# Retention in a hybrid decoder block: the queries made by seven products, and the sums of seven products made in PSUM

## The chip, the cores and the metric

One core of a Trainium2 chip runs the whole program in one launch. The metric is the device time of one execution in microseconds, with data already in the chip's memory; lower is better. The core has a matrix engine (TensorE, PE in the profile, whose weight loads stand in a row of their own, PEld), two element-wise engines that can read the matrix engine's result banks (VectorE, DVE; ScalarE, ACT), a third that can't (GpSimd, POOL), and a queue that issues most of the DMAs (SyncE, SP). Matrix products land in PSUM, eight banks of 512 numbers per partition; everything else lives in SBUF, 128 partitions wide.

## The reference

A block of a decoder: 512 tokens and 16 learned meta tokens ahead of them, width 1024. The mixers share one normalised input `hn` and one wide projection. The change is in retention, the first of the two mixers (4 heads, keys and queries 256 wide, values and gates 512 wide):

```python
proj = hn @ w_in
rq, rk, rv, rg, ... = split(proj)
q_r = rotary(heads(rq), pos) * RET_DK ** -0.5
k_r = rotary(heads(rk), pos)
y_ret = head_groupnorm(retention(q_r, k_r, heads(rv)))    # scores with a decay, times values
y_ret = (silu(rg) * merge_heads(y_ret)) @ w_ret_out
y_sb  = stick_breaking(sq, sk, sv) @ w_sb_out
merged = sigmoid(ga) * y_ret + sigmoid(gb) * y_sb
h = h + rmsnorm(merged @ w_out)
h = h + rmsnorm(swiglu(rmsnorm(h)))
```

## The kernel before, in words

**Precision.** Each operand of a product is kept as two parts, a high part in a reduced 32-bit type and the remainder (`split`, lines 103 to 108: ScalarE copies to the high part, VectorE subtracts it to get the low one). Each product is three matrix instructions per 128 rows of the inner dimension: high by high, high by low, low by high. Weights come by DMA in pieces of 512 KB (`raw_of`, line 118, four buffers named `raw`), are split into `wh` and `wl` (five pairs of buffers), and are used once.

**Seven products.** Most projections are made by the seven products of Strassen and Winograd: the weights are cut into quarters a11, a12, a21, a22, the 512 tokens and the 1024 features likewise into b11 to b22. Sums of weight quarters s1 to s4 are made by GpSimd for each piece of weights (`tok_quarters`, line 238, for tokens on the partitions; `feat_quarters`, line 221, for features on them, four operations of 128x512 at line 230; the results lie in two buffers named `st`). Sums of token quarters t1 to t4 (`th`, `tl`) are made once. The seven products are a11 b11, a12 b21, s2 t2, s3 t3, s1 t1, s4 b22 and a22 t4, and the four quarters of the result are sums of them:

- q11 = a11 b11 + a12 b21
- q12 = a11 b11 + s2 t2 + s1 t1 + s4 b22
- q21 = a11 b11 + s2 t2 + s3 t3 + a22 t4
- q22 = a11 b11 + s2 t2 + s3 t3 + s1 t1

In `seven` (line 263) every product has PSUM columns of its own. ScalarE copies the first to the SBUF tile `ub` (line 269), and VectorE adds the others to it in four steps (lines 274, 277, 280, 285). `tok_seven` (line 297) does this for tokens on the partitions, with 24 matrix instructions of 256 columns to a product; `feat_seven` (line 287), used in the FFN, for features on the partitions, with 12 of 256 columns.

**Retention, head by head** (line 1111). For each of the four heads: queries and keys (`ret_qk`, line 990), scores, gate (`ret_gate`, line 1072), scores times values with the normalisation (`ret_pv`), transposes of the gated result (`ret_T`), values of the next head (`rv_proj`, line 943), and the output projection (`ret_out`). Values and gate are made by seven products. The queries are made plainly: 8 steps of the inner dimension by 3 instructions by 2 halves of the 256 features, 48 instructions of 512 columns, straight into a pair of PSUM banks from which `rotate` (line 971) reads them. The keys need the meta tokens too, 528 columns in two parts of 264, and are plain.

**PSUM** in this stage: two tiles of two banks (`pa`), two of one bank (`pp`), two of one bank (`pb`).

**Order.** A scheduler places the instructions of this stage on each engine ahead of time: in the program each engine has one fixed list, and runs it in order. An instruction whose data are not there holds up all that stand behind it on its engine. Matrix instructions of different stages are interleaved in PE's list. SyncE's list holds the weight loads; each waits for a free `raw` buffer.

Of the kernel before, what the change touches and what calls it, by code (L numbers as in the profile page):

```python
# [16 lines left out]
P = 128  # L17
# [17 lines left out]
def hybrid_block(  # L35
# [106 lines left out]
    def feat_mm(dst, unit, xh, xl, kn=KD):  # L142

        wh, wl = unit
        for k in range(kn):
            mm(dst, wh[:, k, :], xh(k), start=(k == 0), stop=False)
            mm(dst, wh[:, k, :], xl(k), start=False, stop=False)
            mm(dst, wl[:, k, :], xh(k), start=False, stop=(k == kn - 1))

    def tok_mm(dst, units, xh, xl, first=True, last=True, k0=0):  # L150
# [3 lines left out]
        for wh, wl in units:  # L154
            for kk in range(wh.shape[1]):
                k = k0 + i
                mm(dst, xh(k), wh[:, kk, :], start=(first and i == 0), stop=False)
                mm(dst, xh(k), wl[:, kk, :], start=False, stop=False)
                i += 1
                mm(dst, xl(k), wh[:, kk, :], start=False, stop=(last and i == n))  # L160
# [60 lines left out]
    def feat_quarters(src, sums, pin=False):  # L221
# [12 lines left out]
        a, b, c, d = wun_split(raw1), wun_split(x), wun_split(y), wun_split(A22)  # L234
# [3 lines left out]
    def tok_quarters(src, sums=None):  # L238
# [6 lines left out]
        if sums is None:  # L245
# [5 lines left out]
            u["s2"], u["s3"], u["s1"], u["s4"] = [wun_split(a) for a in (A11, A21, A22, A12)]  # L251
# [7 lines left out]
        u["s2"], u["s3"], u["s1"] = wun_split(x), wun_split(y), wun_split(A21)  # L259
# [37 lines left out]
    def tok_seven(u, tok, ub, **kw):  # L297


        def product(n, dst):  # L300
            a, b = PRODUCTS[n]
            xh, xl = tok.operand(b)
            wh, wl = u[a]
            for s in range(2):
                ts_ = slice(s * P, (s + 1) * P)
                tok_mm(dst[:, s * 256 : (s + 1) * 256], [(wh, wl)], lambda k: xh(k)[:, ts_], lambda k: xl(k)[:, ts_])

        one = iter([bank_p, bank_p, bank_b])
        seven(product, lambda: next(one)(), bank_a, ub, **kw)
# [612 lines left out]
    s4.tile([P, 4, 512], F32, tag="ub", name="ub", bufs=1)  # L922
# [20 lines left out]
    def rv_proj(h):  # L943
        u = tok_quarters(w_in[:, O_RV + DV * h : O_RV + DV * (h + 1)], s4 if h else None)
        ub = s4.tile([P, 4, 512], F32, tag="ub", name="ub", bufs=1)
# [14 lines left out]
        tok_seven(u, tokens, ub, after=meta_part)  # L960
        vh = s4.tile([P, NT, DV], F32R, tag="vh", name="vh", bufs=1)
        vl = s4.tile([P, NT, DV], F32R, tag="vl", name="vl", bufs=1)
        for q in range(4):
            c, t = q // 2, q % 2
            dst = lambda v: v[:, 2 * t : 2 * t + 2, 256 * c : 256 * (c + 1)]
            split(dst(vh), dst(vl), ub[:, q, :].rearrange("p (a b) -> p a b", a=2))
# [23 lines left out]
    def ret_qk(h):  # L990
        uq = feat_units(w_in[:, O_RQ + DK * h : O_RQ + DK * (h + 1)])
# [399 lines left out]
```

## Time and profile before

| | |
|---|---|
| median of 3 runs | 1178.63 us (1178.5 to 1179.28) |
| profiled execution, own time | 1178.72 us |
| its span, first to last instruction | 1176.9 us |
| PE busy | 1164.9 us, 7529 matrix instructions |
| DVE, ACT, POOL busy | 844.0, 532.1, 333.5 us |
| TensorE clock granted | 0.999 of full speed |

The span is what the trace covers; 1.8 us of the execution's own time lie around it. A row of the timeline gives the start from the span's begin and the duration; a group gives its count, its summed and mean duration, and the idle time of the engine just before it with what ended that. The start of retention is at 331.5 us, its heads last some 104 us each, and the FFN's products run from some 840 to 1000 us. PE's rows overlap, since matrix instructions are pipelined: a group's mean duration (0.28 us at 256 columns) is longer than the distance from one start to the next, and it is the distance that adds up to time.

### The profile page before, as it was taken

What the parts mean: (1) busy time and instruction counts of PE and PEld (TensorE: products, weight loads), DVE (VectorE), ACT (ScalarE), POOL (GpSimd) and SP (SyncE); (2) the same over time, 40 slices, a digit from 0 to 9 for tenths busy, and PEclk for the clock granted to TensorE, in tenths of its full rate; (3) what the DMA queues carried; (4) which work ended last, traced back from release to release, by engine and by line L of the source; (5) the groups of instructions that cost most, each with busy time, mean ns of one, the idle gap of its engine ahead of it and who ended that gap; (6) DMA issues with size and microseconds to landing.
All of it is one profiled execution on the core that took longest, in us unless ns stands there. A gap on an engine that the chain in (4) does not pass through costs nothing.

```text
span 1176.9 us, 18856 instructions
## 1 busy us (share of the span) xinstructions
PE 1164.9 (99%) x7529; PEld 1056.3 (90%) x7529; DVE 844.0 (72%) x1120; ACT 532.1 (45%) x899; POOL 333.5 (28%) x358
## 2 busy tenths in 40 slices
PE   9999999999999999999999999999999999999997
PEld 7988999988899998998899898888999999998886
DVE  7488888888577873786586567767799998773333
ACT  6476666666233434434243334335455444442321
POOL 2021112126644403320240200001356676610000
PEclk9999999999999999999999999999999999999999
DMA  7332122222641323115122434344033333353311
GB/s 235 99 99 74 62 72 64 77 77 92 194 148 60 93 90 114 55 53 154 36 82 82 133 90 134 126 160 126 19 108 108 109 108 108 108 162 101 97 36 72
DMA packets 146536, 118.25 MB, mean 100 GB/s; under 512 B 3832, under 2 KB 135168, under 8 KB 146448
## 3 DMA queue, kind: packets, MB, share of 16 engines
q1 hardware_dynamic: 145856, 115.85, 32.5%
q8 instruction: 59, 0.97, 0.4%
q10 hardware_dynamic: 592, 1.20, 0.3%
q14 instruction: 29, 0.24, 0.1%
HBM read 109.96 MB, written 7.08 MB: 99 GB/s over the span
## 4 chain that ended last, share of the span: by engine, by line
PE 92%; DVE 5%; issue 1%; ACT 1%; DMA 0%; POOL 0%; POOLq 0%; DVEq 0%; ACTq 0%
PE pp L95 41%; PE pb L95 20%; PE pa L95 20%; PE pc L95 5%; PE px L95 3%; PE pb L98 3%; DVE wl L101 1%; DVE sm L603 1%; ACT wh L104 1%; DVE sl L101 0%; DMA ysb<-in_x_dram 0%; DVE al L101 0%; DVE kl L101 0%; DVE qb L101 0%; DVE qa L101 0%
## 5 line engine op out<-in xcount | busy, mean ns | idle before, releaser
L101 DVE TENSOR_TENSOR wl<-raw,wh 128x1024 fp32r<-128x1024 f32 x196 | 260.7, 1338 | 60.3 <-ACT wh L104 59.3
L104 ACT ACTIVATE wh<-raw 128x1024 fp32r<-128x1024 f32 x194 | 195.2, 1014 | 203.4 <-PE pa L95 59.5
L95 PE MATMUL pp<-hT,wh 128*128 128x512 f32 (+1 forms) x304 | 112.0, 369 | 0.0
L95 PE MATMUL pp<-hL,wh 128*128 128x512 f32 (+1 forms) x304 | 107.7, 354 | 0.0
L95 PE MATMUL pp<-hT,wl 128*128 128x512 f32 (+1 forms) x304 | 107.6, 354 | 0.0
L258 POOL TENSOR_TENSOR st<-raw 128x512 f32<-128x512 f32 x28 | 44.4, 1608 | 170.3 <-DMA raw<-in_w_in_dram 170.3
L101 DVE TENSOR_TENSOR wl<-st,wh 128x1024 fp32r<-128x1024 f32 x54 | 75.1, 1392 | 13.1 <-ACT wh L104 12.1
L95 PE MATMUL pp<-qk,wh 128*128 128x512 f32 x256 | 80.1, 394 | 0.0
L230 POOL TENSOR_TENSOR st<-raw 128x512 f32<-128x512 f32 x40 | 61.1, 1528 | 50.3 <-DVE wl L101 50.3
L95 PE MATMUL pp<-wh,hT 128*128 128x256 f32 (+1 forms) x240 | 73.9, 309 | 0.1
L95 PE MATMUL pp<-wl,hT 128*128 128x256 f32 (+1 forms) x240 | 73.0, 305 | 0.7 <-DVE wl L101 0.4
L95 PE MATMUL pp<-wh,hL 128*128 128x256 f32 (+1 forms) x240 | 73.0, 305 | 0.2 <-DVE hL L101 0.2
L104 ACT ACTIVATE wh<-st 128x1024 fp32r<-128x1024 f32 x54 | 56.6, 1056 | 35.6 <-PE pp L95 15.6
L95 PE MATMUL pa<-hL,wh 128*128 128x264 f32 (+1 forms) x208 | 66.2, 318 | 0.0
L95 PE MATMUL pa<-hT,wh 128*128 128x264 f32 (+1 forms) x208 | 66.2, 318 | 0.0
L95 PE MATMUL pa<-hT,wl 128*128 128x264 f32 (+1 forms) x208 | 66.1, 318 | 0.0
L603 DVE TENSOR_TENSOR_SCAN sm<-sm,mask 128x528 f32<-128x528 f32 (+1 forms) x64 | 54.8, 857 | 14.3 <-ACT sm L600 13.5
L95 PEld LDWEIGHTS pp<-hT,wl 128*128 128x128 f32 x304 | 57.2, 188 | 8.4
L613 POOL CAST mg<-sp 128x32 fp32r<-128x32 f32 x32 | 7.5, 233 | 197.6 <-DVE sp L604 153.7
L95 PEld LDWEIGHTS pp<-hT,wh 128*128 128x128 f32 x304 | 57.3, 188 | 5.8
L95 PEld LDWEIGHTS pp<-hL,wh 128*128 128x128 f32 x304 | 57.4, 189 | 5.3
L95 PEld LDWEIGHTS pp<-qk,wh 128*128 128x128 f32 x256 | 47.7, 188 | 10.7
(346 smaller groups left out, 3680.3 us busy)
## 6 DMA issues: line engine op xcount, KB each, us to landing
raw<-in_w_in_dram SPq DMA_DIRECT2D x88, 512.0 KB, 4.2
raw<-in_w_ffn_in_dram SPq DMA_DIRECT2D x44, 512.0 KB, 3.8
raw<-in_w_ffn_out_dram SPq DMA_DIRECT2D x22, 512.0 KB, 3.6
raw<-in_w_ret_out_dram SPq DMA_DIRECT2D x16, 512.0 KB, 3.4
raw<-in_w_sb_out_dram SPq DMA_DIRECT2D x8, 512.0 KB, 3.9
raw<-in_w_out_dram SPq DMA_DIRECT2D x8, 512.0 KB, 4.0
ysb<-in_x_dram SPq DMA_DIRECT2D x4, 512.0 KB, 7.1
gb_d<-go SPq DMA_DIRECT2D x8, 256.0 KB, 2.0
```

The source lines that it names most:

```text
L95: return keep(nc.tensor.matmul(*args, **kw))
L98: return keep(nc.tensor.transpose(dst, src, idn))
L101: return nc.vector.tensor_tensor(lo, src, hi.bitcast(F32), op=ALU.subtract)
L104: ins = nc.scalar.activation(hi, src, AF.Copy)
L230: ins = nc.gpsimd.tensor_tensor(d, p, q, op=op)
L258: nc.gpsimd.tensor_tensor(d[:, k : k + 2], p[:, k : k + 2], q[:, k : k + 2], op=op)
L603: nc.vector.tensor_tensor_scan(rev, rev, mask[:, r0:][:, ::-1], 0.0, op0=ALU.mult, op1=ALU.max)
L613: nc.gpsimd.tensor_copy(g[:, two, 0:NM], m)
```

## The change

Three things. First, the queries of each head are made by seven products as well (`feat_quarters` and the new `feat_chain`): 84 instructions of 256 columns in place of 48 of 512. Their weights are loaded as before, GpSimd makes four sums of them (line 230), and three and a half pieces are split in place of two. The result lies in the SBUF tile `ub`, from which `rotate` reads it. The keys' first half stands between the sixth and the seventh product.

Second, in `tok_seven` (values and gate) and in `feat_chain` the sums are made in PSUM: one bank `pa` takes a11 b11, then s2 t2, s3 t3 and a22 t4 on top of it, and is read in between: after a11 b11 (for q11), after s2 t2 (for q12), after s3 t3 (for q22); at the end it is q21. A second bank takes s1 t1 and is copied (for q22), then takes s4 b22 on top and is added to q12. A third takes a12 b21 and is added to q11. ScalarE makes three copies per set, VectorE three additions of one quarter each. PE must hold back the next product into a bank until the reader is done.

Third, each quarter is passed on (`done`) as soon as it is complete; for values and gate q21 is read straight from PSUM. The order in which the sums of weights are split changes (s1 ahead of s3). `seven` and `feat_seven` stay as they are for the FFN. `ub` shrinks from four quarters to three.

```diff
-    def feat_mm(dst, unit, xh, xl, kn=KD):
+    def feat_mm(dst, unit, xh, xl, kn=KD, first=True, **kw):
...
-        a, b, c, d = wun_split(raw1), wun_split(x), wun_split(y), wun_split(A22)
+        a, c, b, d = wun_split(raw1), wun_split(y), wun_split(x), wun_split(A22)
...
-            u["s2"], u["s3"], u["s1"], u["s4"] = [wun_split(a) for a in (A11, A21, A22, A12)]
+            u["s2"], u["s1"], u["s3"], u["s4"] = [wun_split(a) for a in (A11, A22, A21, A12)]
...
-        u["s2"], u["s3"], u["s1"] = wun_split(x), wun_split(y), wun_split(A21)
+        u["s2"], u["s1"], u["s3"] = wun_split(x), wun_split(A21), wun_split(y)
...
-    def tok_seven(u, tok, ub, **kw):
...
-        one = iter([bank_p, bank_p, bank_b])
-        seven(product, lambda: next(one)(), bank_a, ub, **kw)
+    def tok_seven(u, tok, ub, done, after=lambda n: None):
+        def product(name, dst, more=False, last=False):
+            a, b = name
             xh, xl = tok.operand(b)
             for s in range(2):
                 ts_ = slice(s * P, (s + 1) * P)
+                tok_mm(dst[:, s * 256 : (s + 1) * 256], [u[a]], lambda k: xh(k)[:, ts_], lambda k: xl(k)[:, ts_], first=not more and s == 0, last=True, skip_group_check=True)
+
+        def add(d, p):
+            nc.vector.tensor_tensor(d, p, d, op=ALU.add)
+
+        q11, q12, q22 = [ub[:, i, :] for i in range(3)]
+        pa = bank_a()[:, 0, :]
+        product(("a11", "b11"), pa)
+        nc.scalar.activation(q11, pa, AF.Copy)
+        pc = bank_p()
+        product(("a12", "b21"), pc, last=True)
+        after(1)
+        add(q11, pc)
+        done(0, 0, q11)
+        product(("s2", "t2"), pa, True)
+        nc.scalar.activation(q12, pa, AF.Copy)
+        pb = bank_p()
+        product(("s1", "t1"), pb)
+        nc.scalar.activation(q22, pb, AF.Copy)
+        product(("s3", "t3"), pa, True)
+        add(q22, pa)
+        done(1, 1, q22)
+        product(("s4", "b22"), pb, True, True)
+        add(q12, pb)
+        done(0, 1, q12)
+        product(("a22", "t4"), pa, True, True)
+        after(6)
+        done(1, 0, pa)
+
+    def feat_chain(u, tok, q, beside):
+        banks = {}
+
+        def product(name, bank, more=False):
+            a, b = name
+            feat_mm(banks[bank], u[a], *tok.operand(b), KH, first=not more, skip_group_check=True)
...
+        (q11, q12), (q21, q22) = [[q[:, e, H * t : H * (t + 1)] for t in range(2)] for e in range(2)]
+        banks["a"] = bank_a()[:, 0, :H]
+        product(("a11", "b11"), "a")
+        nc.scalar.activation(q11, banks["a"], AF.Copy)
+        banks["b"] = bank_p()[:, :H]
+        product(("s1", "t1"), "b")
+        nc.scalar.activation(q22, banks["b"], AF.Copy)
+        banks["c"] = bank_p()[:, :H]
+        product(("a12", "b21"), "c")
+        add(q11, banks["c"])
+        product(("s2", "t2"), "a", True)
+        nc.scalar.activation(q12, banks["a"], AF.Copy)
+        product(("s4", "b22"), "b", True)
+        add(q12, banks["b"])
+        product(("s3", "t3"), "a", True)
+        add(q22, banks["a"])
+        beside()
+        product(("a22", "t4"), "a", True)
+        nc.scalar.activation(q21, banks["a"], AF.Copy)
...
     def ret_qk(h):
-        uq = feat_units(w_in[:, O_RQ + DK * h : O_RQ + DK * (h + 1)])
-        pq = bank_a()
-        for e in range(2):
-            feat_mm(pq[:, e, :], uq[e], xtok, ltok)
+        uq = feat_quarters(w_in[:, O_RQ + DK * h : O_RQ + DK * (h + 1)], s4)
+        uk = feat_units(w_in[:, O_RK + DK * h : O_RK + DK * (h + 1)])
...
+        pq = s4.tile([P, 3, 512], F32, tag="ub", name="ub", bufs=1)
+        feat_chain(uq, tokens, pq, lambda: keys(0))
...
+        keys(1)
```

Of the scheduler's new lists, three places are shown, two engines at the first and PE at the second. Numbers behind a name tell buffers apart.

ScalarE, where the values of the first head end and its queries begin, before (`wh_4186` and `wh_4190` are the two pieces of query weights, `wh_4265` and `wh_4269` the keys'):

```order
L104 ACTIVATE wh_4186<-raw_4182 128x1024
L104 ACTIVATE vh_4169<-ub_3951 128x2x256
L104 ACTIVATE wh_4190<-raw_4184 128x1024
L104 ACTIVATE vh_4169<-ub_3951 128x2x256
L104 ACTIVATE wh_4265<-raw_4261 128x1024
L104 ACTIVATE wh_4269<-raw_4263 128x1024
```

and now (`st_4186` holds s1 and s4 of the query weights, `st_4185` s2 and s3, both GpSimd's):

```order
L322 ACTIVATE ub_3951<-pa_3955 128x512
L104 ACTIVATE wh_4191<-raw_4181 128x1024
L325 ACTIVATE ub_3951<-pp_4053 128x512
L104 ACTIVATE wh_4195<-st_4186 128x1024
L104 ACTIVATE wh_4199<-st_4185 128x1024
L104 ACTIVATE vh_3953<-ub_3951 128x2x256
L104 ACTIVATE wh_4203<-raw_4183 128x512
```

The splits of the query weights now read GpSimd's sums where they read the DMA's buffers, and they stand ahead of the values' own split.

VectorE at the same place, before:

```order
L274 TENSOR_TENSOR ub_3951<-pa_3979,ub_3951 128x1024
L101 TENSOR_TENSOR wl_4187<-raw_4182,wh_4186 128x1024
L101 TENSOR_TENSOR vl_4170<-ub_3951,vh_4169 128x2x256
L277 TENSOR_TENSOR ub_3951<-pp_4048,ub_3951 128x512
L101 TENSOR_TENSOR wl_4191<-raw_4184,wh_4190 128x1024
L280 TENSOR_TENSOR ub_3951<-pb_4074,ub_3951 128x2x512
```

and now:

```order
L101 TENSOR_TENSOR wl_4192<-raw_4181,wh_4191 128x1024
L101 TENSOR_TENSOR wl_4196<-st_4186,wh_4195 128x1024
L310 TENSOR_TENSOR ub_3951<-pa_3955,ub_3951 128x512
L101 TENSOR_TENSOR wl_4200<-st_4185,wh_4199 128x1024
L101 TENSOR_TENSOR vl_3954<-ub_3951,vh_3953 128x2x256
L310 TENSOR_TENSOR ub_3951<-pp_4053,ub_3951 128x512
```

The addition that reads the values' bank (L310, `pa_3955`) stands behind a split of GpSimd's sums.

PE, in the values of the second head, where s2 t2 ends (into `pa_4872`) and s1 t1 or s3 t3 begin; before, the third product had a bank of its own:

```order
L95 MATMUL pa_4872<-wh_4824,th_94 128x256
L95 MATMUL pa_4872<-wl_4825,th_94 128x256
L95 MATMUL pa_4872<-wh_4824,tl_95 128x256
L95 MATMUL pp_4941<-wh_4828,th_94 128x256
L95 MATMUL pp_4941<-wl_4829,th_94 128x256
```

and now (s2 t2 ends in `pa_4906`; then come six of s1 t1 in `pp_5004`, eight transposes of the gated result, and s3 t3 into `pa_4906` again):

```order
L95 MATMUL pa_4906<-wh_4882,tl_95 128x256
L95 MATMUL pp_5004<-wh_4886,th_94 128x256
L95 MATMUL pp_5004<-wl_4887,th_94 128x256
L95 MATMUL pp_5004<-wh_4886,tl_95 128x256
L95 MATMUL pp_5004<-wh_4886,th_94 128x256
L95 MATMUL pp_5004<-wl_4887,th_94 128x256
L95 MATMUL pp_5004<-wh_4886,tl_95 128x256
L98 MATMUL pb_4838<-ident_73,g_4560 128x128 x4
L98 MATMUL pb_4847<-ident_73,g_4560 128x128 x4
L95 MATMUL pa_4906<-wh_4890,th_94 128x256
```

The bank of s2 t2 is written again 14 instructions after it was complete; ScalarE reads it in between.

57 lines of the change are left out of this document (26 added, 31 removed).

## The prediction, on record before the run

> **What bounds the kernel now.** The page comes first: the busy line of PE and the chain that ended last, by engine.
>
> ```profile
> span 1176.9 us, 18856 instructions
> PE 1164.9 (99%) x7529; PEld 1056.3 (90%) x7529; DVE 844.0 (72%) x1120; ACT 532.1 (45%) x899; POOL 333.5 (28%) x358
> PE 92%; DVE 5%; issue 1%; ACT 1%; DMA 0%; POOL 0%; POOLq 0%; DVEq 0%; ACTq 0%
> ```
>
> PE sets the end. Whether it does so in retention, and how far the other engines are from doing it, is read from the busy times of three stretches: the first head, a stretch of only 512-column instructions, and the FFN's products, all of 256 columns. After each stretch's length stand the busy time and the number of instructions of PE, PEld, DVE, ACT and POOL.
>
> ```profile
> 331.50:435.60 104.10, 103.97 (x768) 98.71 (x767) 82.96 (x100) 43.08 (x57) 35.23 (x23) 1.00 0.34 102
> 446.00:470.00 24.00, 24.00 (x105) 19.36 (x104) 6.56 (x7) 8.28 (x12) 10.43 (x8) 1.00 0.37 112
> 850.00:1000.00 150.00, 150.00 (x1260) 150.00 (x1259) 139.78 (x135) 72.37 (x92) 98.54 (x61) 1.00 0.36 106
> ```
>
> In the first head PE is idle for 0.13 of 104 us, at full clock. So what the change takes out of PE's list there comes off the end, unless PE then waits; and everything it adds on DVE, ACT and POOL costs only through such a wait.
>
> A busy PE can still be spaced out. The distance of two starts is what counts, and the timeline of PE shows it in a product of 512 columns:
>
> ```profile
> 320.13 0.39 PE L95 MATMUL pp<-yh,wl 128*128 128x512 f32 x1
> 320.36 0.39 PE L95 MATMUL pp<-yh,wh 128*128 128x512 f32 x1
> ...
> 330.58 0.40 PE L95 MATMUL pp<-yh,wl 128*128 128x512 f32 x1
> ```
>
> From 320.13 to 330.58 there are 45 steps: 0.2322 us each. The stretch from 446 agrees: 24 us by 105, less the two that overlap its edges, is 0.233. For 256 columns the stretch from 850 gives 150 us by 1258, 0.1192 (0.1190 if the edges count): half of 0.2322 and 3 ns.
>
> **The change, part by part.** *PE's list.* A head's queries are 48 by 0.2322 = 11.15 us, and become 84 by 0.1192 = 10.01: 1.14 less, 4.6 us in four heads. The edges of the counts move this by 0.1. The products of values and gate are as many as before, only in another order.
>
> *The work of the other engines.* These are the groups of the operations removed and added.
>
> ```profile
> L104 ACT ACTIVATE wh<-st 128x1024 fp32r<-128x1024 f32 x54 | 56.6, 1056 | 35.6 <-PE pp L95 15.6 <-PE pa L95 15.2 <-POOL st L230 1.8
> L269 ACT ACTIVATE ub<-pp 128x256 f32<-128x256 f32 x20 | 7.5, 375 | 22.7 <-DVE gt L1283 22.7
> L269 ACT ACTIVATE ub<-pp 128x512 f32<-128x512 f32 x8 | 4.8, 595 | 0.2
> L101 DVE TENSOR_TENSOR wl<-st,wh 128x1024 fp32r<-128x1024 f32 x54 | 75.1, 1392 | 13.1 <-ACT wh L104 12.1 <-PE pb L95 0.8
> L274 DVE TENSOR_TENSOR ub<-pa,ub 128x1024 f32<-128x1024 f32 x8 | 9.7, 1211 | 0.8 <-PE pa L95 0.8
> L277 DVE TENSOR_TENSOR ub<-pp,ub 128x256 f32<-128x256 f32 x20 | 8.5, 423 | 1.8
> L277 DVE TENSOR_TENSOR ub<-pp,ub 128x512 f32<-128x512 f32 x8 | 5.5, 685 | 0.1
> L230 POOL TENSOR_TENSOR st<-raw 128x512 f32<-128x512 f32 x40 | 61.1, 1528 | 50.3 <-DVE wl L101 50.3
> L230 POOL TENSOR_TENSOR st<-st,raw 128x512 f32<-128x512 f32 x20 | 26.2, 1311 | 25.8 <-issue 25.7
> L230 POOL TENSOR_TENSOR st<-raw,st 128x512 f32<-128x512 f32 x20 | 44.5, 2227 | 0.0
> ```
>
> VectorE: each set of values or gate gave three steps of 1.21 and one of 0.685, 4.32 us, and now has three of 0.685, 2.06; two sets a head save 4.5. The queries add 1.5 splits of 1.39 and three additions of 0.42, 3.4. Net 1.1 less of 83 a head. ScalarE: two more copies of 0.595 in each of two sets, four of 0.375 and 1.5 splits of 1.06: 5.5 more on 43. GpSimd: four sums, 1.53 + 1.31 + 1.53 + 2.23 = 6.6 more on 35. None of the three fills its 104 us. DMA is unchanged: the query weights come in the same two pieces. What matters is order, at these places.
>
> *The first head's start.* There the query weights have had no time to come early. Four rows of PE, and SyncE's load of the second piece with the VectorE operations that free its buffer:
>
> ```profile
> 331.52 0.28 PE L95 MATMUL pp<-wh,hT 128*128 128x256 f32 x1
> 339.18 0.28 PE L95 MATMUL pa<-wl,th 128*128 128x256 f32 x1
> 335.40 4.43 DVE L101 TENSOR_TENSOR wl<-raw,wh 128x1024 fp32r<-128x1024 f32 x2
> 339.86 5.63 SPq L121 DMA_DIRECT2D raw<-in_w_in_dram  x3
> DMA to landing us min/median/max: 5.4/5.4/5.4
> ```
>
> The load goes out at 339.86, as the split ends (335.40 + 4.43), and takes 5.4 us: 345.26. Nothing ahead of it changes. Before, ScalarE could split the piece at once. Now GpSimd first makes four sums: 5.24 us if all run like the fastest row (1.31), 6.6 by their means, 8.9 if all run like the slowest (2.23). I take 5.9, the middle of the first two, since VectorE does little then: to 351.2. Then the split on ScalarE (1.06), its low part on VectorE (1.39) and, behind it in VectorE's list, the addition that reads the values' bank (0.69): 354.4. PE may write a22 t4 into that bank only then. It arrives there after 180 instructions from 331.52, at 331.52 + 180 by 0.1192 = 352.98, if nothing stops it. **It waits 1.5 us** (0.8 by the fastest, 2.1 by the means, 4.5 by the slowest). Part of this falls earlier: s1 t1 now comes where s2 t2 came, at 339.18 its second instruction needs the low split that ends at 339.83, and PE waits 0.7 there; this only brings forward a part of the same wait.
>
> The Trainium skill, "SBUF — State Buffer", section "Who interferes with whom", says that a VectorE instruction with two inputs in SBUF and a GpSimd instruction that reads SBUF block each other, and one with an input in PSUM does not. The pair at 335.40, 2.2 us each against a mean of 1.39, agrees, as GpSimd ran then. By that rule only one of the four sums would meet such a split here, and the wait would be some 0.3 us longer.
>
> *The values of heads 2 to 4, s3 t3.* PE may go on in the bank of s2 t2 when ScalarE has copied it. ScalarE's list has a split ahead of that copy: 1.06 + 0.6 us after the product's last result, which comes 0.28 after its start: 1.94, less some 0.1 by which ScalarE's operations overlap. PE has six instructions (0.72 with the last of s2 t2's own 0.12 on top, 0.84) and eight transposes:
>
> ```profile
> 429.87 0.60 PE L98 MATMUL pb<-ident,g 128*128 128x128 f32 x4
> 430.23 0.36 PE L95 MATMUL pa<-wh,tl 128*128 128x256 f32 x1
> 430.43 0.64 PE L95 MATMUL pp<-qk,wh 128*128 128x512 f32 x2
> ```
>
> Four take 0.36, eight 0.72: PE is there at 1.56 and waits 0.25. Three times: 0.75 (0 to 1.2).
>
> *A wait that may go.* In three heads PE now waits for one score's decay multiplication before the second output tile:
>
> ```profile
> 405.52 0.28 PE L95 MATMUL pp<-wh,hL 128*128 128x256 f32 x1
> 405.62 0.25 DVE L1041 TENSOR_TENSOR tm<-pb,dec 128x128 f32<-128x128 f32 x1
> 405.93 0.50 PE L95 MATMUL pb<-rvm,smt 80*128 80x512 f32 x1
> ...
> 613.52 0.28 PE L95 MATMUL pp<-wh,hL 128*128 128x256 f32 x1
> 613.77 0.50 PE L95 MATMUL pb<-rvm,smt 80*128 80x512 f32 x1
> ```
>
> The distance is 0.41 at the first and 0.25 at the last, where 0.12 would do: 0.29 and 0.13, some 0.6 in three heads. VectorE is relieved of the long steps there, and the place is rearranged. I take half, 0.3 (0 to 0.6).
>
> *Where a wait is expected to stay hidden.* In the later heads the queries' sums are made during the output projection of the head before, 96 instructions of 512 columns, 22 us.
>
> ```profile
> 437.01 1.50 SPq L121 DMA_DIRECT2D raw<-in_w_in_dram  x2
> ```
>
> If the second query piece is loaded at 437.0 as now, its sums are there at 437.0 + 5.4 + 5.9 = 448.3, and both splits of sums on ScalarE at 450.4. The output projection, which began at 430.43, now has the 56 instructions of values and meta tokens (6.7 us) ahead of it that stood in it: it begins at 437.1. In the new list s2 t2 comes after five of its eight products (60 by 0.2322 = 13.9) and 12 narrow ones (1.4): 452.4. Two microseconds to spare: the estimate is zero. `rotate` now reads SBUF and starts after the last addition; keys' instructions (48 by 0.12) lie between it and the scores, as before.
>
> Sum, against the profiled execution's own 1178.72 (0.1 above the median of the three): 1178.72 - 4.6 + 1.5 + 0.75 - 0.3 = **1176.1 us**. A measurement here tells about 0.2% from no change, 2.4 us: the forecast lies on that border.
>
> **The rivals.**
>
> *All hidden.* The sums run at 1.31 and the wait for the old score goes whole: 0.8 + 0 - 0.6, so 1178.7 - 4.4 = 1174.3. For it: VectorE has less to do, PE's list is free of waits before. Against: the chain of the first head leaves 0.8 even so. Chance 0.22.
>
> *The sums in every head.* The chain load, four sums, split, low split, addition ends after PE's arrival in heads 2 to 4 too: the two spare microseconds are used up if the load goes out 2 us later or the sums take the slowest row's 2.23 (3 us more, so 1 us of waiting a head). Three heads by 1 us: 1179.1, no change. For it: a split that waits for GpSimd holds up ScalarE's copies that free PE's banks. Chance 0.18.
>
> *The same, on the other side.* If the raw buffers are freed so late that each head pays what the first does by the means, 2.1, and the gate's six sums behind the four are pushed as far: 4 by 2.1 twice, so 1178.7 - 4.9 + 0.75 + 16.8 = 1191; with the gate's sums hidden, 1183. It turns at some 1.2 us of waiting a head, 4.9 in all. Against: GpSimd is busy 35 of 104 us. Chance 0.08, with 1183.
>
> *Narrow instructions not worth half.* Each needs its own weight load, and a head's queries load 84 in place of 48. Should an instruction of 256 columns cost over 11.15 / 84 = 0.133 us, the queries lose; at 0.15, 84 by 0.15 is 12.6, and four heads are 5.8 slower instead of 4.6 faster: 1186.5. The stretch from 850 speaks against it, with weight loads busy all the time and 0.119 all the same. Chance 0.01. The Trainium skill, "TensorE: Matmul & The Clock Gate", section "Back-to-back issue gap", gives this rule: in a stream of pairs of load and matmul, 81 ns at 128 columns and 131 at 512. By an estimate on a line between them 256 columns cost 98, and the queries would go from 48 by 131 to 84 by 98, 1.9 us more a head; the rows here (0.232 and 0.119) disagree with the page.
>
> **How the numbers follow.** The forecast has 0.51, with a range of its own of 1175.3 to 1177.2. Half of it lies below 1176.3, the border; with the first rival that is 0.46 for faster. The other half, and the second rival, give 0.45 for the same; the two others 0.09 for slower. The range from 1174.0 to 1179.0 leaves out the slower cases and the far end of the second rival, and takes in the bounds of the first head's wait up to 4.5 us (1179.1).
>
> **What would show it.** In the changed profile: 36 and 48 narrow instructions a head in the query groups; a distance of 0.119 between them; 1.5 us of PE idle or gaps between 339 and 355, ended by VectorE's addition; GpSimd's four sums at L230 from 345.3 to 351; three gaps of 0.25 after the transposes; no gap at the second output tile. It is wrong if PE has gaps in the queries of heads 2 to 4, or if the gate's products wait for their splits.

## The result, and the profile after

The changed kernel takes 1186.2 us (five executions, 1183.79 to 1187.99) against 1178.71 before: a ratio of 1.006, 95% interval 1.0044 to 1.0077. It is slower by 0.6%, and 1176.1 had been forecast, in a range up to 1179.0. Its executions lie further apart than those of before, since the clock granted to TensorE differs between them: three at 0.997 took 1186.2 us and more, two at 0.999 some 1184. The profiled execution is one of the former, 1187.44 us with a span of 1185.6: 8.7 us above that of before.

The page of the changed kernel, the busy times and the chain that ended last:

```profile
span 1185.6 us, 19232 instructions
PE 1165.2 (98%) x7673; PEld 1062.9 (90%) x7673; DVE 843.5 (71%) x1132; ACT 547.7 (46%) x939; POOL 367.7 (31%) x374
PE 81%; DVE 9%; issue 3%; ACT 3%; DMA 2%; POOL 2%; POOLq 0%; DVEq 0%; ACTq 0%
```

PE is as busy as before, but it was to lose 4.6 us, and the span grew by 8.7. VectorE has 9% of the chain where it had 5. So PE waits, and it waits for VectorE. The three stretches of the prediction, in the same columns (length, then busy time and count of PE, PEld, DVE, ACT and POOL, clock, DMA share, GB/s):

```profile
331.50:435.60 104.10, 101.00 (x795) 97.87 (x794) 80.88 (x105) 50.34 (x72) 41.96 (x27) 1.00 0.32 97
446.00:470.00 24.00, 24.00 (x135) 20.80 (x134) 5.82 (x6) 10.00 (x16) 4.31 (x4) 1.00 0.20 65
850.00:1000.00 150.00, 148.54 (x1236) 147.51 (x1235) 130.44 (x126) 70.09 (x92) 91.89 (x57) 1.00 0.34 99
```

The first head is now idle for 3.1 us of 104 on PE. The third stretch is the surprise: it lies in the FFN, and there 1236 instructions run in the time in which 1260 ran before. Who is waited for in retention, from the view of waits of PE (total, number, longest; an idle time counts from the end of the instruction before, 0.28 us after its start, so each is 0.16 more against a distance of 0.12):

```profile
PE pa L95 <- DVE rt L1039: 5.3, 4, 2.1
PE pa L95 <- DVE ub L310: 0.8, 1, 0.8
PE pp L95 <- DVE wl L101: 0.5, 1, 0.5
```

The two lower lines were forecast: the addition that frees the values' bank in the first head, and the split brought forward to s1 t1. The first was not. It is this place, once in each head; the timeline of PE in the second head:

```profile
489.21 0.28 PE L95 MATMUL pp<-wl,th 128*128 128x256 f32 x1
489.33 0.28 PE L95 MATMUL pp<-wh,tl 128*128 128x256 f32 x1
491.71 0.36 PE L95 MATMUL pa<-wh,hT 128*128 128x256 f32 x1 [2.10 <-DVE rt L1039]
```

From 489.33 to 491.71 are 2.38 us where 0.12 would do: a wait of 2.26. The instruction at 491.71 is the gate's a11 b11. It goes into the pair of banks that held the first half of the keys, and L1039 is the last operation that reads it, in the keys' rotation. The four waits are 1.83, 2.26, 1.11 and 0.79, 6.0 us.

What follows the second is in the windows behind it:

```profile
490.00:491.50 1.50, 0.00 (x0) 0.00 (x0) 1.50 (x4) 0.25 (x1) 0.00 (x0) 1.00 0.00 0
491.50:493.00 1.50, 1.29 (x7) 1.32 (x8) 1.50 (x3) 0.78 (x2) 0.00 (x0) 0.68 0.00 0
493.00:494.00 1.00, 1.00 (x7) 1.00 (x6) 1.00 (x3) 1.00 (x2) 0.00 (x0) 0.50 0.00 0
494.00:495.00 1.00, 1.00 (x7) 1.00 (x7) 1.00 (x2) 0.29 (x1) 0.00 (x0) 0.50 0.51 94
```

The granted clock, ahead of the last two columns, is 0.5 to 0.7 until 495, and 0.78 in the microsecond behind. The instructions of this stretch come 1.6 us later than at the full pace.

In the FFN, PE and VectorE, at the start of its first whole set of products:

```profile
908.50 0.28 PE L95 MATMUL pb<-tl,wh 128*128 128x256 f32 x1
910.24 0.38 PE L95 MATMUL pb<-th,wl 128*128 128x256 f32 x1 [1.46 <-DVE wl L101]
...
1001.65 0.28 PE L95 MATMUL pb<-tl,wh 128*128 128x256 f32 x1
1001.82 0.39 PE L95 MATMUL pb<-th,wl 128*128 128x256 f32 x1
...
906.54 1.21 DVE L101 TENSOR_TENSOR wl<-st,wh 128x1024 fp32r<-128x1024 f32 x1
908.01 2.18 DVE L101 TENSOR_TENSOR wl<-st,wh 128x1024 fp32r<-128x1024 f32 x1
```

PE stands in s2 t2, whose third instruction needs the low part of s2. Of the two splits on VectorE, the one at 906.54 is that of s1 and s4, and the one at 908.01 that of s2 and s3: `feat_quarters`, which the FFN shares, has its order changed too, while `feat_seven` still takes s2 t2 third. That costs 1.62 us once, and about 0.16 in every later set (at 1001.82 it is 0.05, and 0.1 at the restart behind it), 3.7 us in all.

The sum, in the profiled execution, for each term:

| term | forecast | measured |
|---|---|---|
| queries in narrow instructions | -4.6 | -4.6 (84 at 0.119 a head) |
| first head, 0.70 at s1 t1 and 0.94 before a22 t4 | +1.5 | +1.8 with 0.1 at each restart |
| s3 t3 in three heads | +0.75 | +1.1 (0.26 each, and 0.1 at the restart) |
| old waits at the second output tile | -0.3 | -1.0 (gone) |
| keys' rotation before the gate | 0 | +6.0 |
| clock behind the second of these | 0 | +1.6 |
| order of the splits in the FFN | 0 | +3.7 |
| sum | -2.65 | +8.6 |

The span grew by 8.7. PE's list lies 4.9 us behind that of before from 850 to 899 us (0.2 of it from ahead of retention) and 8.7 behind from 1035 on, so the rows down to the clock and the FFN's row each fit by themselves, too.

### The profile page after: what moved, and what is told of

It is laid out like the page before. It is cut to its first block, busy times and chain, and to the rows that moved or that the text cites. A ratio compares the mean times of both kernels' runs of the same rounds, so it can differ in the third digit from the quotient of the medians.

```text
span 1185.6 us, 19232 instructions
## 1 busy us (share of the span) xinstructions
PE 1165.2 (98%) x7673; PEld 1062.9 (90%) x7673; DVE 843.5 (71%) x1132; ACT 547.7 (46%) x939; POOL 367.7 (31%) x374
## 4 chain that ended last, share of the span: by engine, by line
PE 81%; DVE 9%; issue 3%; ACT 3%; DMA 2%; POOL 2%; POOLq 0%; DVEq 0%; ACTq 0%
PE pp L95 39%; PE pb L95 18%; PE pa L95 13%; PE pc L95 5%; DVE wl L101 3%; PE px L95 3%; PE pb L98 2%; ACT wh L104 2%; DMA raw<-in_w_in_dram 2%; DVE sm L659 1%; POOL ts L196 1%; DVE qk L101 1%; POOL st L230 1%; DVE rt L1039 0%; DVE rt L1035 0%
## 5 line engine op out<-in xcount | busy, mean ns | idle before, releaser
L95 PE MATMUL pp<-hT,wh 128*128 128x512 f32 (+2 forms) x336 | 121.1, 360 | 0.0
L230 POOL TENSOR_TENSOR st<-raw 128x512 f32<-128x512 f32 x48 | 75.8, 1583 | 133.3 <-DVE wl L101 60.2
L95 PE MATMUL pp<-hL,wh 128*128 128x512 f32 (+2 forms) x336 | 116.6, 347 | 0.0
L95 PE MATMUL pp<-hT,wl 128*128 128x512 f32 (+2 forms) x336 | 116.5, 347 | 0.0
L95 PE MATMUL pp<-wh,hT 128*128 128x256 f32 (+1 forms) x304 | 91.8, 303 | 0.0
L95 PE MATMUL pp<-wl,hT 128*128 128x256 f32 (+1 forms) x304 | 91.0, 300 | 0.7 <-DVE wl L101 0.4
L95 PE MATMUL pp<-wh,hL 128*128 128x256 f32 (+1 forms) x304 | 91.3, 301 | 0.2 <-DVE hL L101 0.2
L258 POOL TENSOR_TENSOR st<-raw 128x512 f32<-128x512 f32 x28 | 44.1, 1597 | 70.5 <-DMA raw<-in_w_in_dram 65.7
L95 PEld LDWEIGHTS pp<-wl,hT 128*128 128x128 f32 x304 | 57.2, 188 | 3.8 <-DVE wl L101 1.4
L95 PEld LDWEIGHTS pp<-wh,hT 128*128 128x128 f32 x304 | 57.3, 188 | 3.3 <-DVE mix L1249 0.4
L95 PEld LDWEIGHTS pp<-wh,hL 128*128 128x128 f32 x304 | 57.2, 188 | 2.6 <-DVE hL L101 0.4
```

What stands on the lines that cost most here:

```text
L95: return keep(nc.tensor.matmul(*args, **kw))
L230: ins = nc.gpsimd.tensor_tensor(d, p, q, op=op)
L258: nc.gpsimd.tensor_tensor(d[:, k : k + 2], p[:, k : k + 2], q[:, k : k + 2], op=op)
```

## The experiments

Times are medians beside runs of the kernel before on the same chip (1178.7 to 1179.0). Where waits are quoted they are PE's, in retention, from the view of waits.

### The FFN: one line in each direction

*e1_split_order*, the kernel before with the new order:

```diff
-        a, b, c, d = wun_split(raw1), wun_split(x), wun_split(y), wun_split(A22)
+        a, c, b, d = wun_split(raw1), wun_split(y), wun_split(x), wun_split(A22)
```

> The kernel before with one line changed: the sums s1 and s4 of the FFN's weights are split ahead of s2 and s3. My theory: the FFN's third product, s2 t2, then waits for its split once at its start and by some 0.3 us in every set after that, and loses the 3.7 us that the changed kernel lost between 757 and 1179 us: 1178.7 + 3.7 = 1182.4 us. Rival: the FFN only lost its place against the DMAs because retention ended later; then the line alone costs nothing: 1178.7 us.

1182.91 us, ratio 1.0036 (1.0024 to 1.0048): 4.2 more. The line alone costs it, with no other edit. PE shows the same wait at the same place:

```profile
905.33 0.39 PE L95 MATMUL pb<-th,wl 128*128 128x256 f32 x1 [1.48 <-DVE wl L101]
```

*e2_ffn_order*, the changed kernel with the new order for the queries alone:

```diff
+        if chain:
             a, c, b, d = wun_split(raw1), wun_split(y), wun_split(x), wun_split(A22)
+        else:
+            a, b, c, d = wun_split(raw1), wun_split(x), wun_split(y), wun_split(A22)
```

> The changed kernel with the old order of the splits in the FFN alone. My theory: 3.7 us come back, 1186.2 - 3.7 = 1182.5 us, or 1180.3 where the clock does not dip. Rival (order not to blame): 1186.2 us.

1183.51 us (1180.89 to 1184.58), 2.7 less than the changed kernel; the clock scatters both. The FFN's stretch is back at 1260 instructions, and the waits before the gate stay (0.83, 2.70, 1.11 and 0.78 us by distance, 5.4 in place of 6.0):

```profile
850.00:1000.00 150.00, 150.00 (x1260) 150.00 (x1259) 138.27 (x133) 74.09 (x94) 97.74 (x60) 1.00 0.35 103
...
PE pa L95 <- DVE rt L1042: 4.8, 4, 2.5
```

All that follows has this edit, unless it starts from the kernel before.

### Which half of the change makes the rotation late

*e4_plain_queries*: `ret_qk` of the kernel before, so that only the sums in PSUM of values and gate are left.

```diff
-        feat_chain(uq, tokens, pq, lambda: keys(0))
+        pq = bank_a()
+        for e in range(2):
+            feat_mm(pq[:, e, :], uq[e], xtok, ltok)
```

> The changed kernel with the queries made plainly, as before, and the old order in the FFN: of the change, the sums in PSUM of values and gate are left. My theory (the queries' sums make the rotation late): PE does not wait for the rotation; nothing is gained and the waits before s3 t3 stay, 1178.7 + 1.2 = 1179.9 us. Rival (the gate's chain in the pair of banks is to blame): the four waits stay, 1178.7 + 1.2 + 5.4 = 1185.3 us.

1179.39 us, ratio 1.0004 (0.9996 to 1.0013). The waits before the gate are gone, though its chain lies in the same pair of banks:

```profile
PE pp L95 <- DVE wl L101: 0.5, 1, 0.5
PE pp L95 <- ACT wh L104: 0.3, 1, 0.3
```

*e5_only_queries*: the other half, `feat_chain` for the queries in the kernel before (the opposite diff).

> The kernel before with the queries alone made by seven products in PSUM; values, gate and FFN as before. PE's list comes to the pair of banks of the keys after as many instructions as in the changed kernel. If the queries' sums make VectorE's rotation late (my theory), the wait stays though the gate's sums are the old ones: 1178.7 - 4.6 + 6.0 = 1180.1 us, up to 1182 with a low clock. If the gate's chain in the pair of banks is to blame (rival), it goes, and the queries' gain is left: 1174.1 us.

1186.11 us, 4 to 6 more than expected. The rotation is waited for in each head (2.5 us in all), and PE also waits at a dozen other places; of those that the view of waits names all but one are for VectorE, among them 1.3 and 1.4 for additions of the output projection. So the queries make the rotation late with the old sums, too. That the sums in PSUM relieve VectorE at the other places is likely, but no run shows it by itself.

### Where the wait goes when one thing is taken away

*e3_gate_bank*: the gate's chain in a single bank, and s1 t1 in the pair, one product later.

```diff
-        pa = bank_a()[:, 0, :]
+        pa = bank_p() if swap else bank_a()[:, 0, :]
...
-        pb = bank_p()
+        pb = bank_a()[:, 0, :] if swap else bank_p()
```

> As the kernel with the old order in the FFN, and the gate's long chain of sums lies in one of the two single banks; the pair that the keys' rotation still reads is needed one product later, for s1 t1. My theory: the four waits for the rotation (1.83 + 2.26 + 1.11 + 0.79 = 6.0 us) go, and with them the 1.6 us in which the clock was low: 1178.7 - 4.6 + 1.7 (first head) + 1.2 (s3 t3) = 1177.0 us. Rival: VectorE's list is late as a whole, and the wait only moves to the scores behind it: 1182 us.

The median is 1180.73 us, but the runs lie between 1177.9 and 1187.6, with clocks from 1.000 down to 0.993; the profiled one took 1177.9. In it PE waits elsewhere:

```profile
PE pb L95 <- DVE tm L1103: 2.6, 3, 1.0
```

This is the scores' decay multiplication. The wait for the bank has gone and half of it has come out a step later: between theory and rival.

*e12_gate_bank_again*, the same kernel, for its clock:

> The kernel with the gate's chain in another bank, once more, for its clock: its runs lie between 1177.9 and 1187.6 us with granted clocks of 1.000 to 0.993. If a wait of PE near 2 us is what lowers the clock (my theory), a profile at 1181 us or more shows such a wait ahead of each stretch of low clock, and one at 1178 shows neither. Rival: the clock falls without a wait.

1178.48 us at full clock, with waits like those above, none over 1.2 us. That fits the theory, but an execution at low clock of this kernel was not seen in a profile, so what lowered it there is open.

*e6_rotate_first*: the splits of the gate's sums are held behind the queries' rotation.

```diff
-        u["s2"], u["s1"], u["s3"] = wun_split(x), wun_split(A21), wun_split(y)
+        u["s2"], u["s1"], u["s3"] = wun_split(x, behind), wun_split(A21, behind), wun_split(y, behind)
-        u["s4"], u["a22"] = wun_split(A12), wun_split(A22)
+        u["s4"], u["a22"] = wun_split(A12, behind), wun_split(A22, behind)
...
-        us = tok_quarters(w_in[:, O_RG + DV * h : O_RG + DV * (h + 1)], s4)
+        us = tok_quarters(w_in[:, O_RG + DV * h : O_RG + DV * (h + 1)], s4, behind)
```

> The changed kernel with the old order in the FFN, and the splits of the gate's sums may stand only behind the copy of the queries' last quarter (ScalarE) and behind the last addition of the queries' rotation (VectorE). My theory (the rotation waits in VectorE's list behind a split that waits for GpSimd): the four waits of the kernel with the old order alone, 0.83 + 2.70 + 1.11 + 0.78 = 5.4 us, shrink to 0.5 in all, and the 1.6 us of low clock go: 1178.7 - 4.6 + 1.8 (first head) + 1.2 (s3 t3) + 0.5 = 1177.6 us. Rival: VectorE has too much to do there whatever comes first, and PE then waits for the splits of the gate's sums: 1181 to 1183 us.

1188.86 us: 5 worse, where 6 better was expected, and above the rival's 1183 as well. The theory behind it came from the changed kernel's VectorE in the first head:

```profile
374.14 1.23 DVE L101 TENSOR_TENSOR wl<-st,wh 128x1024 fp32r<-128x1024 f32 x1 [3.53 <-ACT wh L104]
...
377.52 0.68 DVE L1035 TENSOR_TENSOR rt<-ub,sinT 128x512 f32<-128x512 f32 x1
...
385.69 0.69 DVE L1039 TENSOR_TENSOR rt<-pa,sinT 128x528 f32<-128x528 f32 x1
```

A wait of 3.53 us for the gate's sums, ahead of the queries' rotation, looks like the cause. With the hold, the rotation does start 3.5 us earlier (374.01), but the held splits then stand in the middle of the keys' rotation, and VectorE comes to its last reading at 385.79, as late as before. In the waits' view:

```profile
PE pa L95 <- DVE rt L1043: 6.8, 4, 1.8
PE pb L95 <- DVE qk L101: 2.1, 2, 1.1
```

*e8_four_rt*: the rotation reads its first half twice at once, with a fourth buffer for it.

```diff
-    RT = 3
+    RT = 4
...
         nc.vector.tensor_tensor(t1, x1, c, op=ALU.mult)
+        t3, t4 = tmp(), tmp()
+        nc.vector.tensor_tensor(t3, x1, s, op=ALU.mult)
         nc.vector.tensor_tensor(t2, x2, s, op=ALU.mult)
```

> The changed kernel with the old order in the FFN, four buffers for the rotation's intermediate results in place of three, and the rotation reads its first half twice at once, so that the first half of the keys' banks is free before VectorE turns to the second. My theory: the bank is free before PE comes, the waits of 5.4 us and the low clock go, 1177.1 us. Rival: as the kernel with the gate's chain in another bank, the delay moves on to the scores (3 us there): 1180 us.

1182.51 us. No wait for the bank is left, and the rival is right in the place and size of the wait: PE now waits for the rotated keys, 2.9 us at the scores. The time is 2.5 us above its price.

```profile
PE pb L95 <- ACT qk L104: 1.8, 3, 0.7
PE pb L95 <- DVE qk L101: 1.1, 3, 0.4
```

*e9_no_query_sums*: the four sums on GpSimd are left out, and the splits read the loaded pieces (the queries are then not the reference's).

```diff
+        if chain:
+            x, y = raw2, raw1
...
-        for d, p, q, op in ((S1, A21, A22, ALU.add), (S2, S1, A11, ALU.subtract), (S3, A11, A21, ALU.subtract), (S4, A12, S2, ALU.subtract)):
+        for d, p, q, op in () if chain else ((S1, A21, A22, ALU.add), (S2, S1, A11, ALU.subtract), (S3, A11, A21, ALU.subtract), (S4, A12, S2, ALU.subtract)):
```

> The changed kernel with the old order in the FFN, and GpSimd makes no sums of the queries' weights: the splits read the loaded pieces themselves. This leaves out the four sums of each head, so the queries are not the reference's; everything else is done, the three and a half splits and the additions too. My theory (the sums hold the loaded pieces, so that the gate's weights, GpSimd's sums of them and the rotation come late): the four waits of 5.4 us go, the first head's wait of 1.15 and the low clock too: 1178.7 - 4.6 + 0.7 + 1.2 = 1176.0 us. Rival (VectorE's additional splits and additions are enough for the delay): the waits stay, 1182.5 us.

1180.16 us, between the two. The first head loses its waits before a22 t4 and before the gate; in the other three the rotation is still waited for:

```profile
PE pa L95 <- DVE rt L1044: 3.7, 3, 2.0
```

So GpSimd's sums cause these two waits of the first head, and not the rotation's in the other three. The first head's wait at s1 t1 stays.

*e13_keys_after*: the keys' first half is written behind the queries' seventh product.

```diff
-        beside()
         product(("a22", "t4"), "a", True)
         nc.scalar.activation(q21, banks["a"], AF.Copy)
+        beside()
```

> The changed kernel with the old order in the FFN, and the keys' first half is written behind the queries' seventh product and not ahead of it. On PE the seventh product, a22 t4, comes ten instructions earlier for it (1.2 us); the keys' others still fill the place where it waits for the addition of s3 t3. My theory (the rotation is late because the queries are complete late, behind 48 instructions of keys, and VectorE then has both rotations and the splits to do before PE comes to the gate): each of the waits of 0.83, 2.70, 1.11 and 0.78 us shrinks by up to 1.2, 1.5 us are left, and the low clock goes: 1178.7 - 4.6 + 1.8 + 1.2 + 1.5 = 1178.6 us. Rival (the start of the rotation does not matter, only what stands in VectorE's list): 1183.5 us.

1183.82 us, the rival's time, though the start of the rotation does matter: the wait before the gate shrinks from 4.8 to 2.9 us. That is less than expected, and 2.6 us of new ones appear. Part of the reason is in the second head, VectorE and then GpSimd:

```profile
473.50 1.78 DVE L1038 TENSOR_TENSOR rt<-ub,sinT 128x512 f32<-128x512 f32 x1
475.20 1.77 DVE L1042 TENSOR_TENSOR rt<-ub,sinT 128x512 f32<-128x512 f32 x1
...
474.69 3.44 POOL L261 TENSOR_TENSOR st<-raw 128x512 f32<-128x512 f32 x2
```

And the kernel before, in the third head, also with GpSimd at work:

```profile
575.25 0.68 DVE L978 TENSOR_TENSOR rt<-pa,sinT 128x512 f32<-128x512 f32 x1
...
573.60 2.55 POOL L258 TENSOR_TENSOR raw<-raw,st 128x512 f32<-128x512 f32 x2 [9.30 <-DVE wl L101]
```

While GpSimd works, the same multiplication takes 0.68 us when its input lies in PSUM and 1.78 when it lies in the SBUF tile `ub`. Earlier in the list more of the queries' rotation falls under GpSimd's sums for the gate: seven of its sixteen multiplications take 1.8 us here, two in e2_ffn_order and none in the changed kernel. The Trainium skill, "SBUF — State Buffer", section "Who interferes with whom", says that a VectorE instruction with two inputs in SBUF contends with a GpSimd instruction that reads SBUF, and one with at most one such input does not; the rows agree with it.

### Two edits together, and the fastest version

*e7_all*: the edits of e6_rotate_first and e8_four_rt, the first head's split behind the values' addition, and the splits of s4 and a22 behind ScalarE's copy of q12.

```diff
-            a, c, b, d = wun_split(raw1), wun_split(y), wun_split(x), wun_split(A22)
+            a, c, b, d = wun_split(raw1), wun_split(y, (None, marks["q22"])), wun_split(x), wun_split(A22)
...
-        nc.scalar.activation(q12, pa, AF.Copy)
+        copied = nc.scalar.activation(q12, pa, AF.Copy)
+        if "rest" in u:
+            u.pop("rest")(copied)
```

> The last two edits together, and two more: the split of the queries' sums in the first head stands behind the values' last addition on VectorE, and the splits of s4 and a22 stand behind ScalarE's copy of q12. My theory: the first head's wait of 1.0 before a22 t4 and the three of 0.28 (0.38 with the start that follows) go too, the 0.7 at s1 t1 stays: 1178.7 - 4.6 + 0.7 = 1174.8 us, faster than both kernels. Rival: each wait that goes lets the next one out (scores, copies of the banks): 1178 us.

1176.24 us, ratio 0.9975 (0.9965 to 0.9984): faster than both kernels. Of the waits these are left:

```profile
PE pb L95 <- DVE yn L1140: 0.7, 2, 0.4
PE pp L95 <- DVE wl L101: 0.5, 1, 0.5
PE pa L95 <- DVE ub L356: 0.3, 1, 0.3
```

*e11_no_hold*: the same without the hold, the edit that alone made it worse.

```diff
-        u["s2"], u["s1"], u["s3"] = wun_split(x, behind), wun_split(A21, behind), wun_split(y, behind)
+        u["s2"], u["s1"], u["s3"] = wun_split(x), wun_split(A21), wun_split(y)
```

> The kernel with all four edits, without the one that holds the splits of the gate's sums behind the queries' rotation. My theory (the early reads free the bank, but only together with the hold is the rotation ready for the scores): the 1.6 us a head before the scores come back in three heads: 1176.2 + 4.5 = 1180.7 us. Rival (the hold does nothing, as it did nothing good alone): 1176.2 us.

1180.36 us, as expected. The wait for the rotated keys at the scores is back (two of 0.8 us and one of 0.2), and those for the normalisation grow to 1.3. With the hold alone (e6_rotate_first) PE waited for the bank and another 2.1 us at the scores; with the early reads alone (e8_four_rt) 2.9 at the scores. With both, neither wait is left. The kernel without the early reads alone was not run.

*e10_in_order*: in the first head PE's s1 t1 and its share for the meta tokens stand behind s2 t2, as before the change.

```diff
-        product(("s1", "t1"), pb)
+        product(("s1", "t1"), pb, prev=None if had_rest else prev)
```

> The kernel with all four edits, and in the first head s1 t1 and the meta tokens' product with s1 stand behind s2 t2 on PE, as before the change. My theory: the 0.8 us at s1 t1 go, and nothing later depends on it: 1176.2 - 0.8 = 1175.4 us. Rival: the wait for the queries' sums in the first head comes out in its place: 1176.2 us.

1176.02 us, ratio 0.9978 (0.9968 to 0.9987). The 0.7 at s1 t1 is gone, and 0.5 come out before the gate in the same head:

```profile
PE pa L95 <- DVE rt L1053: 0.5, 1, 0.5
PE pb L95 <- DVE yn L1146: 0.3, 1, 0.3
```

*e14_keys_after_all*: this with the edit of e13_keys_after. It differs from e10_in_order in more than that: the condition on s1 t1 asks `marks` for a name that it never holds, so s1 t1 stands behind s2 t2 in every set and not in the first head's values alone, and the meta tokens' share is not held.

```diff
-        product(("s1", "t1"), pb, prev=None if had_rest else prev)
+        product(("s1", "t1"), pb, prev=None if "rest" in marks else prev)
```

> The kernel with all the edits and the first head's order, and the keys' first half behind the queries' seventh product as well. My theory: nothing there waits for long any more, so only the 0.6 us before the gate in the first head can go: 1175.4 to 1176.0 us. Rival (PE comes to the scores and to the gate's bank earlier than the rotation): 1178 us.

1186.88 us (1183.74 to 1188.49), with granted clocks of 0.997 to 0.994; the profile is of the fastest.

```profile
PE pa L95 <- DVE rt L1051: 5.9, 3, 2.4
```

In the last three heads PE comes to the gate's a11 b11 directly behind the keys' second half, and waits there 2.6, 1.9 and 1.9 us for the rotation. In e13_keys_after, with the keys at the same place, 24 instructions of the gate's a12 b21 and 9 of its s1 t1 stood between; in e10_in_order six of s1 t1 did, and a12 b21 stood ahead of the keys. Now s1 t1 may not come ahead of a11 b11, and the scheduler has moved a12 b21 as well. PE does come earlier than the rotation, as the rival says, but the run does not tell how much of the 11 us the keys' place costs and how much the hold on s1 t1.

## Why the prediction was wrong

**What bounds the kernel** was read rightly: PE, and waits of PE for other engines are what counts.

**The narrow queries** bring what was forecast: a product of 12 in the changed kernel runs from 358.72 to 360.03 in eleven steps, 0.119 each, and the sum closes with 4.6. The estimate of 98 ns from the Trainium skill, "TensorE: Matmul & The Clock Gate", section "Back-to-back issue gap", and the loss of 1.9 us a head that would follow from it do not hold here.

```profile
358.72 0.28 PE L95 MATMUL pp<-th,wh 128*128 128x256 f32 x1
...
360.03 0.28 PE L95 MATMUL pp<-th,wl 128*128 128x256 f32 x1
```

**The first head's start**, 1.5 us, and **s3 t3**, 0.75, were right in mechanism and near in size (1.8 and 1.1). What both missed is the restart: after a wait the second instruction comes 0.22 us behind the first in place of 0.12, so a wait costs 0.1 more than it lasts. Three details of the working are off by little. Its own terms for the first head add up to 1.4 us and not 1.5. Eight transposes take 0.87 us (0.109 from one to the next), not 0.72. And the two splits of the pair at 335.40 took 3.30 and 1.21 us, not 2.2 each: the long one ran beside GpSimd's operation of 334.35 to 337.62, the short one behind it. The queries' sums in the first head ran from 345.67 to 351.80; three took 1.28 or 1.29 us and one, beside a split, 2.27. **The wait at the second output tile** went whole and not by half.

**The step that failed** is "Where a wait is expected to stay hidden", in its last sentence: "`rotate` now reads SBUF and starts after the last addition; keys' instructions (48 by 0.12) lie between it and the scores, as before." Two things are wrong in it, and one was left open. First, half of the keys' instructions stand ahead of the queries' last product now. The rotation's operation that needs the last quarter ran at 367.22 in the first head, and runs at 377.52; even where nothing stands ahead of it (e6_rotate_first) it runs at 374.01. From there VectorE has to do both rotations and the gate's splits in one go. Second, the first to wait is not the scores but the gate's first product, which needs the keys' bank; before, that bank was free 2.4 us ahead of its use (the first row is the query's operation of before, on VectorE, the second the last reading of the keys' bank):

```profile
367.22 0.68 DVE L978 TENSOR_TENSOR rt<-pa,sinT 128x512 f32<-128x512 f32 x1
...
380.22 0.70 DVE L982 TENSOR_TENSOR rt<-pa,sinT 128x528 f32<-128x528 f32 x1
...
383.34 0.28 PE L95 MATMUL pa<-wh,hT 128*128 128x256 f32 x1
```

Third, "reads SBUF" was noted and not priced. In the changed kernel's profile this cost nothing at that place: of the sixteen multiplications of the queries' rotation twelve took 0.68 us and one 0.70, as from PSUM, and the three longer ones (1.33, 1.00, 0.99) came 16 us and more ahead of the wait. It adds to e2_ffn_order and e13_keys_after. The two spare microseconds of that step were worked out for the queries' sums alone, at the start of the head, and for these they held.

That the queries and no other part make the rotation late is shown (e4_plain_queries and e5_only_queries). What makes it late within them is shown in part. Kernels that take one thing away, GpSimd's sums (e9), the keys ahead of the last product (e13) or the splits ahead of the rotation (e6), keep a wait for the rotation; kernels that free the bank earlier or need it later (e8, e3) move a good half of the wait to the scores. How the 6.0 us divide among the causes was not settled.

The signs that the prediction named all came: 0.119 between narrow instructions, the four sums, the wait ended by VectorE's addition, the short gaps behind the transposes, none at the second output tile. Its two signs of being wrong did not: PE has no gap in the queries of heads 2 to 4, and the gate's product waits for its bank and not for its splits. The wait lay where it had named no sign.

**The rival on the other side** had 0.08, with 1183 us. Without the FFN's loss that is what was measured (1183.5, e2_ffn_order). The agreement is luck, since its mechanism holds only in part: the gate's weights do come late (GpSimd's sums for it start at 361.5 in place of 354.6 in the first head), but without the queries' sums three of the four waits stayed.

**What had no term at all** is the FFN. The description of the change says that its functions stay as they are, and the working follows the split order only into retention, although `feat_quarters` is called from both. One line of the diff was worth 3.7 us in the profile, 4.2 by itself (e1_split_order), nearly half of the loss. **The clock** had none either.

## What to carry to other kernels

When a helper changes, list its callers, and at each compare the order in which it now delivers with the order in which the caller takes. For each bank, find who reads it last and who writes it next, and work out both times anew when work is added to the reader's engine: the first to wait need not be the step that uses the result. If a wait moves when one of its causes is removed, that cause was one of several that lie close together, and edits that fail alone (here +5 us and -1 us against e2_ffn_order) can win together (-7, with two smaller ones).

## What the runs showed of the hardware

A PE wait of 2.26 us in the changed kernel was followed by 3.4 us at half clock, which cost 1.6 more. In e6_rotate_first a wait of 1.96 had the same sequel, and two of 1.89 had not. One of 2.56 in e14_keys_after_all and one of 2.20 in e9_no_query_sums left the clock at full speed; the windows around the latter, where PE is idle from 590.6 to 592.7:

```profile
588.00:592.00 4.00, 2.62 (x22) 2.42 (x21) 3.92 (x5) 1.58 (x2) 2.74 (x2) 1.00 0.01 2
592.00:593.00 1.00, 0.33 (x3) 0.36 (x4) 1.00 (x2) 0.00 (x0) 0.00 (x0) 1.00 0.00 0
593.00:594.00 1.00, 1.00 (x11) 1.00 (x10) 1.00 (x2) 0.82 (x2) 0.00 (x0) 1.00 0.00 0
```

The length of the wait alone does not decide it. In each trace the granted clock changes only at whole steps of 3.413 us from one change to the next: in the changed kernel it is 1.00 from 488.62 to 492.03, 0.50 from 492.03 to 495.45 and 1.00 behind. With each trace cut at such steps, these are the stretches that hold most of the longer waits in retention, by the time that PE was busy in them:

| run | stretch, us | PE busy in it, us | wait, us | clock in the next stretch |
|---|---|---|---|---|
| e2_ffn_order | 488.57 to 491.99 | 0.88 | 2.70 | 0.50 |
| after | 488.62 to 492.03 | 1.31 | 2.26 | 0.50 |
| e6_rotate_first | 489.88 to 493.30 | 1.62 | 1.96 | 0.50 |
| e14_keys_after_all | 691.24 to 694.65 | 1.63 | 1.95 | 0.50 |
| e9_no_query_sums | 588.95 to 592.36 | 1.68 | 2.20 | 1.00 |
| e14_keys_after_all | 585.43 to 588.84 | 1.73 | 1.93 | 1.00 |
| e14_keys_after_all | 483.03 to 486.44 | 1.90 | 2.56 | 1.00 |
| e6_rotate_first | 595.70 to 599.11 | 2.21 | 1.89 | 1.00 |

In these rows up to 1.63 us of work in a stretch were followed by half clock, and 1.68 or more were not. The wait of 2.56 us lies across the edge of two stretches, that of 1.95 in one. Where the steps lie differs from trace to trace, so a wait of some 2 us can cost 1.6 more in one execution and nothing in another. That this makes the executions of one kernel scatter by several microseconds is likely, but no kernel was profiled both with and without the low clock.

The Trainium skill, "TensorE: Matmul & The Clock Gate", section "What's actually happening", says that the clock is halved after an idle window of about 3.4 us and that the windows run freely. The length of the low stretch agrees; the wait that was enough for it is shorter than stated.
